# A hybrid decoder layer: the x1 transposes in the out projection and the first half of the MoBA keys' transposes move to other places

## The chip, the cores and the metric

The kernel runs on one NeuronCore of one Trainium2 chip. The metric is the device time of one execution in microseconds (us), the median of the runs. Lower is better.

## The reference

One decoder layer on a 256 x 1024 input. The projection `h @ w_in` gives queries, keys and values for two attention mixers (NSA with its compressed, selected and window branches, and MoBA), and gates; what the two mixers give is merged by gates and `w_out`, and a feed-forward part follows. The parts that the change touches:

```python
qkv = qkv_m.reshape(b, seq, 3, MOBA_HEADS, d)
qm = partial_rope(qkv[:, :, 0], cos, sin)
km = partial_rope(qkv[:, :, 1], cos, sin)
vm = qkv[:, :, 2]
y_moba = moba_attention(to_kv(qm), to_kv(km), to_kv(vm))
...
mixed = g_nsa * (y_nsa @ w_up_nsa[layer]) + g_moba * (y_moba @ w_up_moba[layer])
x = x + mixed @ w_out[layer]
h2 = rmsnorm(x, norm2_g[layer])
u = jax.nn.relu(h2 @ w_ff1[layer])
x = x + (u * u) @ w_ff2[layer]
```

With 256 tokens a MoBA block is the whole sequence, so MoBA is causal attention over 8 heads of 64.

## The kernel before

**Weights in 60 chunks.** All weights pass through in chunks of about 1 MB. Chunk c has a slot, slot c, in which TensorE (PE) multiplies with it. Each weight is split into two fp32r parts: ACT writes `whi`, a rounded copy (line 100), and DVE writes `wlo`, the rest (line 102). In slot c the split of chunk c+2 runs, in two halves (`split`), and SP's queue loads chunk c+5 (`load`). There are three buffers each of `raw`, `whi` and `wlo`.

**Triples of passes.** `mm3` makes three matmuls for each product: high by high, high by low, low by high; the first two have the same operand as weights. Here each of the three is called a pass. In slots 0 to 11 (`xstat`) the activations `hTh` and `hTl` are the weights and 512 columns of a chunk stream by: 24 passes a slot, numbered from 0, in triples (hTh, whi), (hTh, wlo), (hTl, whi). In the slots behind (`wstat`) the chunk's columns are the weights: (whi, high), (whi, low), (wlo, high), 48 passes of 256 columns a slot.

**Order by hand.** The program is written out in the order in which it is to run on each engine. `at(pos, f, ...)` puts a piece of other work at a share of a slot; `run_slot` sorts the pieces by share and issues each before the first pass i with pos <= i/n, where n is the number of passes. So pos 0.25 of 24 is ahead of pass 6, pos 0.48 ahead of pass 12. Every engine works off its own queue in that order; where one engine needs what another makes, it waits at the head of its queue.

**Slots 8 to 12, around the keys.** Slots 8 and 9 make the MoBA keys `km` (in the buffers `qtm`), slots 10 and 11 the values `vm`. The keys are rotated by DVE (`rope`, lines 276 to 279) in the middle of slot 10. In slot 11 `transp_heads` (lines 281 to 296) transposes them in two halves: four PE transposes (line 286) into one PSUM bank, then `split_evac`: ACT copies the bank to `kmh` (line 303) and `km` (line 304), and DVE subtracts to `kml` (line 305). From slot 11 on only the bank `tp` is left for this (`turn["tp"]`), so the two halves share it. The results are first read in slot 17. Also in slot 11, by share of the slot: the halves of the split's `whi` at 0.0 and 0.06 and of `wlo` at 0.09 and 0.46; at 0.1 the scores of attention unit 1 and the products of unit 0 on PE; at 0.11 unit 1's maxima on DVE (`d_max`, lines 440 to 446, first `Sa`, then `Sb`); at 0.12 unit 0's result (`d_yevac`, lines 506 and 507); at 0.5 the exponentials over `Sa` on ACT (`d_exp`, line 453) and the evacuation of the first `vm` bank (line 266); at 0.52 the exponentials over `Sb`. The norm of unit 1 (`d_norm`, line 458) follows in slot 12. Slot 12 begins the merge gates and writes the bank that the first `vm` evacuation frees.

**Slots 24 to 27, the out projection.** Slot 24+i makes two blocks of `mixed @ w_out`; its evacuation (`wout_evac`, lines 702 to 710) stands at the beginning of the next slot: DVE adds the blocks to x in `x1T`. In slot 25 `x1_rows` transposes the first two blocks of `x1T` into the bank `yb` (line 722), and ACT copies them out (line 724).

Of the kernel before, what the change touches and what calls it, by code (L numbers as in the profile page):

```python
# [40 lines left out]
def hybrid_layer(ctx: ExitStack, tc: tile.TileContext, gxd, w, w1c, small, const, gf, out):  # L41
# [14 lines left out]
    def bank(tag, name):  # L56
        return ps.tile([128, 512], F32, name=name, tag=tag)
# [8 lines left out]
    def acc_tile():  # L66
        return next_bank("acc")
# [4 lines left out]
    def s_tile(x):  # L72
        return ps_s.tile([128, 2, 512], F32, name="S" + "ab"[x])
# [113 lines left out]
    def at(pos, f, *a):  # L187
        ev.append((pos, f, a))

    def run_slot(mms):  # L190
        n = len(mms)
        es = sorted(ev, key=lambda e: e[0])
        ev.clear()
        j = 0
        for i, m in enumerate(mms):
            while j < len(es) and es[j][0] <= i / n:
                es[j][1](*es[j][2])
                j += 1
            m()
        while j < len(es):  # L200
            es[j][1](*es[j][2])
            j += 1
# [9 lines left out]
    def xstat(c, n, accs, kts):  # L212

        r = []
        h, l = hi[c], lo[c]
        order = [(t, k) for t in range(2) for k in range(4)]
        if c == 0:
            order.sort(key=lambda e: e[1])
        for t, k in order:
            kt = kts[k]  # L220
            if True:
                lh, ll = (a[:, kt, t * 128:(t + 1) * 128] for a in (hTh, hTl))
                r += mm3(accs[t][:, :n], lh, ll, h[:, k * n:(k + 1) * n],
                         l[:, k * n:(k + 1) * n], kt == 0, kt == 7)
        return r

    def wstat(o, c, off, nk, ncol, ah, al, ks=None, first=0, last=None):

        r = []
        last = nk - 1 if last is None else last  # L230
        for k in (range(nk) if ks is None else ks):
            a = k * ncol + off
            r += mm3(o, hi[c][:, a:a + 128], lo[c][:, a:a + 128], ah[:, k, :], al[:, k, :],
                     k == first, k == last)
        return r

    def split_events(c, hs, ls):
        for i in range(2):
            at(hs[i], split, c + 2, i, 2, "h")
        for i in range(2):  # L240
            if ls[i] <= 1:
                at(ls[i], split, c + 2, i, 2, "l")
        if ls[1] <= 1:
            at(max(ls) + 0.05, load, c + 5)

    def std_events(c):
        if 9 <= c < 20 and c % 2:
            split_events(c, (0.0, 0.06), (0.09, 0.46))
        elif 9 <= c < 20:
            split_events(c, (0.0, 0.45), (0.3, 0.8))  # L250
        else:
            split_events(c, (0.0, 0.45), (0.3, 0.46))
# [6 lines left out]
    tm = {"kva": kva, "kvb": kvb, "vm": vm}  # L259
# [47 lines left out]
    def qk_tiles(name, n, q):  # L307
        m = 128 if q else 256
        return (ap_.tile([128, n, 128], F32, name=name + "0"),
                ap_.tile([128, n, m], F32R, name=name + "h"),  # L310
                ap_.tile([128, n, m], F32R, name=name + "l"))
# [61 lines left out]
    qrT, qmT, kmT = (qk_tiles(n, 4, n != "km") for n in ("qr", "qm", "km"))  # L373
# [135 lines left out]
    def unit_events(s):  # L509
        d = (s - 9) // 2  # L510
        if not 9 <= s <= 21:
            return
        if s % 2 == 0:
            at(0.1, d_norm, d)
            at(0.78, d_trans, d)
            return
        if d < 6:
            at(0.1, d_scores, d)
        if d > 0:
            at(0.1, d_pv, d - 1)  # L520
        if d < 6:
            at(0.11, d_max, d)
            at(0.2 if s > 12 else 0.5, d_exp, d, 0)
            at(0.22 if s > 12 else 0.52, d_exp, d, 1)
        if d > 0:
            at(0.12, d_yevac, d - 1)
# [4 lines left out]
    for sec, c0, n in groups:  # L531
        if sec in ("q", "qm", "km"):
            tm[sec] = ap_.tile([128, 2, 512], F32, name="qtm", bufs=2)
        if sec == "kvb":
            accs = [s_tile(t)[:, 0] for t in range(2)]
        else:
            accs = [acc_tile(), acc_tile()]
        for i in range(2):
            c = c0 + i
            if c == 0:  # L540
                at(0.6, load, 5)
            elif c == 1:
                at(0.87, row_norm)
                for k in range(4):
                    at(0.88, split, 2, k, 4)
                for k in range(4):
                    at(1.1, split, 3, k, 4)
                at(1.2, load, 6)
            elif c == 2:
                split_events(c, (0.0, 0.3), (0.5, 0.8))  # L550
                at(0.3, cmp_gather, 0)
                at(0.55, cmp_gather, 1)
                at(0.7, rope, kva, 2)
            else:
                std_events(c)
            unit_events(c)
            if c == 3:
                at(0.65, cmp_mlp1)
                at(0.85, transp_k, kva, ksT)
            if c == 4:  # L560
                at(0.2, gate_evac)
                at(0.3, rope, kvb[:, :, 0:128], 2)
                at(0.4, cmp_mlp2)
            if c == 5:
                at(0.3, transp_k, kvb[:, :, 0:128], kwT)
            if c == 6:
                at(0.4, transp_heads, tm["q"], qT, 0)
                at(0.5, transp_heads, tm["q"], qT, 1)
                at(0.6, rope, tm["q"], 8)
            if c == 7:  # L570
                at(0.1, cmp_scores)
                at(0.4, transp_heads, tm["q"], qrT, 0)
                at(0.55, transp_heads, tm["q"], qrT, 1)
            if c == 8:
                at(0.35, cmp_probs_t)
                at(0.3, rope, tm["qm"], 8)
            if c == 9:
                at(0.3, transp_heads, tm["qm"], qmT, 0)
                at(0.45, transp_heads, tm["qm"], qmT, 1)
            if c == 10:  # L580
                at(0.5, rope, tm["km"], 8)
            if c == 11:
                turn["tp"] = ["tp"]
                at(0.25, transp_heads, tm["km"], kmT, 0, False)
                at(0.48, transp_heads, tm["km"], kmT, 1, False)
            if i == 1:
                at(1.0 if c == 1 else 0.5, evac_tm, sec, 0, accs[0], n)
                at(1.0, evac_tm, sec, 1, accs[1], n)
            run_slot(xstat(c, n, accs, range(4 * i, 4 * i + 4)))
# [122 lines left out]
    def lo_late(pos, c):  # L712
        for k in range(2):
            at(pos, split, c + 2, k, 2, "l")
        at(pos + 0.01, load, c + 5)

    def x1_rows(k2s, tiles):
        for k2, tp in zip(k2s, tiles):
            v = tp.rearrange("p (t d) -> p t d", t=2)
            for t in range(2):  # L720
                for m in range(2):
                    pe.transpose(v[:, t, m * 128:(m + 1) * 128],  # L722
                                 x1T[:, 2 * k2 + m, t * 128:(t + 1) * 128], ident)
            act.activation(FB["x1"][:, :, k2 * 256:(k2 + 1) * 256], v, AF.Copy)

    for i in range(4):
        c = C_WOUT + i
        if i == 0:
            lo_late(0.03, c - 1)
        split_events(c, (0.0, 0.1), ((0.5, 0.5), (0.3, 0.3), (0.3, 0.3), (9, 9))[i])  # L730
        for f, a in prev:
            at(0.02, f, *a)
        if i == 1:
            at(0.01, open_ff)
            at(0.5, lambda: x1_rows([0], [bank("yb", "yb")]))
            at(0.9, lambda: act.dma_start(FB["gfb"], gf[None, :].to_broadcast([128, 1024])))
        if i == 3:
            outs = [acc_tile()[:, 0:256] for _ in range(2)]
            at(0.52, wout_evac, i, outs, (0,))
            run_slot([m for j in range(2)  # L740
                      for m in wstat(outs[j], c, j * 128, 8, 256, mxh, mxl)])
            prev = [(wout_evac, (i, outs, (1,)))]
        else:
            mms, outs, _ = two_blocks(c, mxh, mxl, 6 if i == 0 else 8)
            run_slot(mms)
            prev = [(wout_evac, (i, outs))]
# [198 lines left out]
```

## Time and profile before

| | us |
|---|---|
| median of 3 runs | 392.18 |
| lowest and highest | 391.62, 392.22 |
| the profiled execution | 392.12 |
| its span, first to last instruction | 390.3 |
| PE busy in it | 377.5 (97%) |

Engines: PE is TensorE's matmul, PEld its weight load, DVE VectorE, ACT ScalarE, SP the queue of the loads. L286 is line 286 of the kernel. A matmul's row is longer than its step, since matmuls overlap: the distance from start to start is what it costs. In the PE rows the operands are named by the program's tiles, `acc<-whi,hTh`; which of them are the weights depends on the slot, as told above. Idle time that a row gives in brackets is that of its engine just before it, with the instruction that ended it.

### The profile page before, as it was taken

What the parts mean: (1) busy time and instruction counts of PE and PEld (TensorE: products, weight loads), DVE (VectorE), ACT (ScalarE), POOL (GpSimd) and SP (SyncE); (2) the same over time, 40 slices, a digit from 0 to 9 for tenths busy, and PEclk for the clock granted to TensorE, in tenths of its full rate; (3) what the DMA queues carried; (4) which work ended last, traced back from release to release, by engine and by line L of the source; (5) the groups of instructions that cost most, each with busy time, mean ns of one, the idle gap of its engine ahead of it and who ended that gap; (6) DMA issues with size and microseconds to landing.
All of it is one profiled execution on the core that took longest, in us unless ns stands there. A gap on an engine that the chain in (4) does not pass through costs nothing.

```text
span 390.3 us, 6512 instructions
## 1 busy us (share of the span) xinstructions
PE 377.5 (97%) x2687; PEld 343.7 (88%) x2687; DVE 261.1 (67%) x400; ACT 204.6 (52%) x358; POOL 10.0 (3%) x18
## 2 busy tenths in 40 slices
PE   6899999989999999999999999999999999999993
PEld 5688888868999999999999999999998888888883
DVE  5987487895978879867957666667567443344444
ACT  5565645747747467526445455555655464334412
POOL 5300000000000000000000000000000000000001
PEclk9999999999999999999999999999999999999998
DMA  7885625333335333632674546445645547455003
GB/s 237 316 346 219 216 107 192 132 107 111 109 109 191 128 115 107 217 118 99 233 252 160 188 196 216 174 158 209 213 145 183 214 154 275 165 177 200 0 2 107
DMA packets 11693, 66.33 MB, mean 170 GB/s; under 512 B 1296, under 2 KB 3600, under 8 KB 4368
## 3 DMA queue, kind: packets, MB, share of 16 engines
q1 hardware_dynamic: 11232, 65.14, 46.5%
q10 hardware_dynamic: 432, 0.79, 0.7%
q8 instruction: 21, 0.34, 0.3%
q14 instruction: 8, 0.07, 0.1%
HBM read 64.87 MB, written 1.05 MB: 169 GB/s over the span
## 4 chain that ended last, share of the span: by engine, by line
PE 87%; DVE 5%; issue 3%; ACT 2%; DMA 1%; SPq 0%; POOL 0%; POOLq 0%; DVEq 0%
PE acc L205 55%; PE o L205 21%; PE yb L205 2%; PE Sb L205 2%; PE Sa L205 2%; DVE wlo L102 1%; ACT P L453 1%; PE tp L205 1%; DMA gx<-in_gx_dram 1%; PE tp L286 1%; PE Sb L479 1%; PE Sa L479 1%; DVE hTl L162 1%; PE acc L722 0%; DVE P L467 0%
## 5 line engine op out<-in xcount | busy, mean ns | idle before, releaser
L100 ACT ACTIVATE whi<-raw 128x1024 fp32r<-128x1024 f32 (+2 forms) x128 | 123.8, 990 | 102.7 <-PE o L205 35.4
L102 DVE TENSOR_TENSOR wlo<-raw,whi 128x1024 fp32r<-128x1024 f32 (+2 forms) x128 | 145.1, 1165 | 43.7 <-ACT whi L100 43.6
L205 PE MATMUL acc<-h2h,whi 128*128 128x256 f32 x256 | 71.9, 281 | 0.0
L205 PE MATMUL acc<-h2l,whi 128*128 128x256 f32 x256 | 71.9, 281 | 0.0
L205 PE MATMUL acc<-h2h,wlo 128*128 128x256 f32 x256 | 71.9, 281 | 0.0
L205 PE MATMUL o<-whi,sqh 128*128 128x512 f32 (+1 forms) x128 | 49.5, 387 | 0.0
L205 PE MATMUL o<-whi,sql 128*128 128x512 f32 (+1 forms) x128 | 49.4, 386 | 0.0
L205 PE MATMUL o<-wlo,sqh 128*128 128x512 f32 (+1 forms) x128 | 49.4, 386 | 0.0
L205 PEld LDWEIGHTS acc<-h2h,whi 128*128 128x128 f32 x256 | 49.2, 192 | 0.0
L205 PEld LDWEIGHTS acc<-h2l,whi 128*128 128x128 f32 x256 | 48.1, 188 | 0.0
L205 PEld LDWEIGHTS acc<-h2h,wlo 128*128 128x128 f32 x256 | 48.0, 188 | 0.0
L205 PE MATMUL acc<-hTh,wlo 128*128 128x256 f32 x128 | 37.3, 291 | 0.0
L205 PE MATMUL acc<-hTh,whi 128*128 128x256 f32 x128 | 36.3, 283 | 0.4 <-ACT vm L266 0.4
L205 PE MATMUL acc<-hTl,whi 128*128 128x256 f32 x128 | 36.1, 282 | 0.0
L205 PE MATMUL acc<-wlo,hTh 128*128 128x512 f32 (+1 forms) x80 | 31.7, 397 | 3.4 <-DVE wlo L102 3.2
L205 PE MATMUL acc<-whi,hTh 128*128 128x512 f32 (+1 forms) x80 | 31.6, 395 | 0.0
L205 PE MATMUL acc<-whi,hTl 128*128 128x512 f32 (+1 forms) x80 | 30.7, 384 | 0.0
L205 PEld LDWEIGHTS o<-whi,sql 128*128 128x128 f32 x128 | 24.0, 188 | 4.9
L205 PEld LDWEIGHTS o<-whi,sqh 128*128 128x128 f32 x128 | 24.0, 188 | 4.9
L205 PEld LDWEIGHTS o<-wlo,sqh 128*128 128x128 f32 x128 | 24.0, 188 | 4.8
L205 PEld LDWEIGHTS acc<-hTh,whi 128*128 128x128 f32 x128 | 24.5, 191 | 0.9 <-ACT vm L266 0.8
L205 PEld LDWEIGHTS acc<-hTh,wlo 128*128 128x128 f32 x128 | 24.4, 191 | 0.8 <-issue 0.7
(243 smaller groups left out, 619.3 us busy)
## 6 DMA issues: line engine op xcount, KB each, us to landing
raw<-in_ff_dram SPq DMA_DIRECT2D x32, 1024.0 KB, 4.8
raw<-in_gm_dram SPq DMA_DIRECT2D x8, 1024.0 KB, 4.8
raw<-in_wout_dram SPq DMA_DIRECT2D x4, 1024.0 KB, 4.8
raw<-in_q_dram SPq DMA_DIRECT2D x2, 1024.0 KB, 6.2
raw<-in_qm_dram SPq DMA_DIRECT2D x2, 1024.0 KB, 5.8
raw<-in_km_dram SPq DMA_DIRECT2D x2, 1024.0 KB, 5.6
raw<-in_vm_dram SPq DMA_DIRECT2D x2, 1024.0 KB, 4.8
raw<-in_upn_dram SPq DMA_DIRECT2D x2, 1024.0 KB, 4.7
```

The lines of the kernel that those rows point to most:

```text
L100: act.activation(hi[c][:, a:b], raw[c][:, a:b], AF.Copy)
L102: dve.tensor_tensor(lo[c][:, a:b], raw[c][:, a:b], hi[c][:, a:b].bitcast(F32), op=ALU.subtract)
L162: dve.scalar_tensor_tensor(hTl[:, kt, :], xT[:, kt, :], g1[:, kt:kt + 1], hTh[:, kt, :].bitcast(F32), op0=ALU.mult, op1=ALU.subtract)
L205: pe.matmul(o, l, r, start=start, stop=stop, skip_group_check=True)
L286: pe.transpose(tp[:, j * 256 + t * 128:j * 256 + t * 128 + 128], src[:, t, (2 * i + j) * 128:(2 * i + j + 1) * 128], ident)
L453: act.activation(P[:, 2 * x + j, a:b], S[x][:, j, a:b], AF.Exp, scale=0.125, bias=st[:, 1, i:i + 1], accum_out=st[:, 2, i:i + 1])
L479: pe.transpose(S[x][:, j, c:c + 128], P[:, 2 * x + j, c:c + 128], ident)
```

## The change

The four x1 transposes of slot 25 move from 0.5 of the slot, ahead of pass 24 (the first of a triple), to 26/48 - 0.001, ahead of pass 26 (behind the second of a triple). The first half of the keys' transposes in slot 11 moves from 0.25, ahead of pass 6, to 0.02, ahead of pass 1: behind the first pass of the slot, behind the first half of the split's `whi`, and now ahead of the second half of `whi`, of both halves of `wlo`, of unit 1's scores and maxima and of unit 0's products and result. With the transposes move their ACT copies and their DVE subtraction. The second half stays at 0.48.

```diff
             if c == 11:
                 turn["tp"] = ["tp"]
-                at(0.25, transp_heads, tm["km"], kmT, 0, False)
+                at(0.02, transp_heads, tm["km"], kmT, 0, False)
                 at(0.48, transp_heads, tm["km"], kmT, 1, False)
...
         if i == 1:
             at(0.01, open_ff)
-            at(0.5, lambda: x1_rows([0], [bank("yb", "yb")]))
+
+            at(26 / 48 - 0.001, lambda: x1_rows([0], [bank("yb", "yb")]))
             at(0.9, lambda: act.dma_start(FB["gfb"], gf[None, :].to_broadcast([128, 1024])))
```

## Rows read from the trace of the kernel before

**Rows 1.** The page: busy us, share and instructions; then its chain by engine

```profile
PE 377.5 (97%) x2687; PEld 343.7 (88%) x2687; DVE 261.1 (67%) x400; ACT 204.6 (52%) x358; POOL 10.0 (3%) x18
...
PE 87%; DVE 5%; issue 3%; ACT 2%; DMA 1%; SPq 0%; POOL 0%; POOLq 0%; DVEq 0%
```

**Rows 2.** Stretches: length, busy us of PE, PEld, DVE, ACT, POOL, clock, DMA

```profile
60.00:92.00 32.00, 30.46 (x188) 24.02 (x187) 25.28 (x52) 19.57 (x50) 0.00 (x0) 1.00 0.44 148
92.00:184.00 92.00, 92.00 (x822) 88.39 (x822) 72.86 (x113) 54.11 (x120) 0.00 (x0) 1.00 0.37 132
184.00:206.00 22.00, 22.00 (x189) 22.00 (x189) 15.93 (x24) 11.21 (x17) 0.00 (x0) 1.00 0.63 216
```

**Rows 3.** Waits: engine, line, releaser: total us, times, longest

```profile
PEld tp L286 <- DVE kml L305: 1.6, 1, 1.6
```

**Rows 4.** Timeline, PE, slot 11: start, us, instruction, out<-in [idle before <-releaser]

```profile
80.47 0.40 PE L205 MATMUL acc<-whi,hTh 128*128 128x512 f32 x1
...
86.44 0.40 PE L205 MATMUL acc<-whi,hTl 128*128 128x512 f32 x1
...
87.96 0.66 PE L286 MATMUL tp<-ident,qtm 128*128 128x128 f32 x4 [1.12 <-DVE kml L305]
...
88.92 0.39 PE L205 MATMUL acc<-whi,hTl 128*128 128x512 f32 x1
...
90.96 0.39 PE L205 MATMUL acc<-whi,hTl 128*128 128x512 f32 x1
...
91.77 0.39 PE L205 MATMUL acc<-hTh,whi 128*128 128x256 f32 x1 [0.41 <-ACT vm L266]
```

**Rows 5.** Timeline, PE, slot 9, around a transposition behind a second pass

```profile
68.22 0.40 PE L205 MATMUL acc<-wlo,hTh 128*128 128x512 f32 x1
...
69.36 0.40 PE L205 MATMUL acc<-wlo,hTh 128*128 128x512 f32 x1
```

**Rows 6.** Timeline, DVE, slots 10 to 12

```profile
79.82 0.29 DVE L279 TENSOR_TENSOR qtm<-ropa,ropb 128x128 f32<-128x128 f32 x1
...
80.90 2.35 DVE L102 TENSOR_TENSOR wlo<-raw,whi 128x1024 fp32r<-128x1024 f32 x2
...
83.17 0.69 DVE L440 TENSOR_TENSOR Sa<-Sa,kc 128x512 f32<-128x512 f32 x1
...
84.95 0.17 DVE L446 TENSOR_SCALAR ust<-ust 128x4 f32<-128x4 f32 x1
...
87.22 0.68 DVE L305 TENSOR_TENSOR kml<-tp,kmh 128x512 fp32r<-128x512 f32 x1
...
89.56 0.69 DVE L305 TENSOR_TENSOR kml<-tp,kmh 128x512 fp32r<-128x512 f32 x1 [0.52 <-ACT km L304]
...
93.35 0.17 DVE L458 TENSOR_SCALAR ust<-ust 128x8 f32<-128x8 f32 x1 [3.10 <-ACT P L453]
```

**Rows 7.** Timeline, ACT, slot 11

```profile
80.71 2.01 ACT L100 ACTIVATE whi<-raw 128x1024 fp32r<-128x1024 f32 x2 [1.47 <-PE acc L205]
...
85.48 0.60 ACT L303 ACTIVATE kmh<-tp 128x512 fp32r<-128x512 f32 x1 [0.94 <-PE tp L286]
...
85.97 0.38 ACT L304 ACTIVATE km<-tp 128x256 f32<-128x256 f32 x1
...
89.41 0.37 ACT L453 ACTIVATE P<-Sa,ust 128x128 f32<-128x128 f32 x1
```

**Rows 8.** Timeline, PE, PEld and DVE, out projection, slot 25

```profile
187.95 0.28 PE L205 MATMUL acc<-mxh,whi 128*128 128x256 f32 x1
...
190.31 0.28 PE L205 MATMUL acc<-mxh,wlo 128*128 128x256 f32 x1
...
191.10 0.28 PE L205 MATMUL acc<-mxh,wlo 128*128 128x256 f32 x1
...
190.33 0.46 PEld L722 LDWEIGHTS yb<-ident,gx 128*128 128x128 f32 x4
...
189.57 0.75 DVE L702 TENSOR_TENSOR gx<-gx,acc 128x256 f32<-128x256 f32 x2
```

## The prediction

> **What bounds the kernel now.** I read the page's busy times and chain first: TensorE is busy for 97% of the span and carries 87% of the chain [rows 1]. So only time in which PE itself stands still, or extra work on PE, can move the end. The stretches then say where it stands still: from 92 to 206 us PE is busy without a gap, from 60 to 92 us it lacks 1.5 us, all at the full granted clock, 1.00 [rows 2]. The waits name the larger gap: the weight loads of the MoBA keys' transposes (line 286) waited once for DVE's `kml` (line 305), 1.6 us [rows 3]. The PE timeline of slot 11 shows it: pass 11 starts at 86.44, then nothing until 87.96, then four transposes; a smaller gap stands at the start of slot 12, at 91.77, behind ACT's evacuation of `vm` [rows 4].
>
> Why PE stood there follows from the two engines that empty the bank. In slot 11 both halves of the keys go through the one bank `tp`. The first half is read out by ACT (`kmh` at 85.48, `km` at 85.97) [rows 7] and by DVE (`kml`), and DVE has `kml` queued behind the whole maximum of the next attention unit, which holds it from 83.17 to 87.22 [rows 6]. The second half's transposes can only start when `kml` is over, at 87.90. They are also at the head of PE's queue, so passes 12 to 23, which need nothing from that bank, wait with them.
>
> **Part 1, the keys' first half, from pass 6 to pass 1 of slot 11.** No instruction is added; four transposes, two ACT copies and one DVE subtraction move forward on their queues, and no DMA is issued by them.
>
> The stall's size: from pass 11 to pass 14 it takes 88.92 - 86.44 = 2.48 us [rows 4]. The same pattern without a wait (three steps and four transposes) is in slot 9: 69.36 - 68.22 = 1.14 [rows 5]. The stall is 1.34 us. One step of a 512-column pass is (90.96 - 88.92)/9 = 0.227 [rows 4], so four transposes cost 1.14 - 3 x 0.227 = 0.46, paid in the old place and in the new one; with the move pass 11 still starts at 86.44.
>
> On PE in the new place: the transposes follow pass 0, at 80.47 + 0.23 = 80.70 [rows 4], their weights a step earlier, at 80.47. They read the rotated keys, whose last DVE instruction ends at 79.82 + 0.29 = 80.11 [rows 6]: 0.36 us to spare. The bank was last used two slots before.
>
> On ACT: the first half of the weights' split stands ahead, from 80.71, 1.0 us a half [rows 7]. Then `kmh` starts at 81.71, `km` at 82.20 and ends at 82.58. The second half of that split goes back by about 0.9 us; it is needed two slots later.
>
> On DVE: `kml` waits for `km` too, as its second instance does (0.52 us for ACT's `km`) [rows 6]. So it runs from 82.61 to 83.29. In the queue it now stands between the two subtractions that begin at 80.90, 2.27 us for both up to 83.17, 1.13 each [rows 6]. The second of them, and the maximum behind it, begin at 83.29 + 1.13 = 84.42 instead of 83.17: 1.25 us later. That is the cost of the move, and it has cover. The first exponentials, which need the maximum of `Sa`, ran at 89.41 [rows 7] because ACT had the second half's copies ahead of them; that maximum's last instruction ends at 84.95 + 0.17 = 85.12 [rows 6], then at 86.37.
>
> What the bank is worth: free at 83.29, it is wanted at 86.44. So the second half's transposes start a step after pass 11, at 86.67, and pass 14 at 88.92 - 1.34 = 87.58. What is late next is the same evacuation of `vm`: behind it are copies and exponentials that all hang on the second half's transposes, and these come earlier by the same amount, so slot 12 begins at 91.77 - 1.34 = 90.43, with its gap as before. The exponentials begin at 89.41 - 1.34 = 88.07, 1.70 us after the delayed maximum. DVE's next work, the norm at 93.35, had waited 3.10 us for ACT [rows 6], so 1.25 us of delay are gone before it. From there on PE has no gap to lose the gain in [rows 2], and DVE and ACT follow PE. SP's load of a later chunk, released by DVE's second subtraction of the slot, may go out about half a microsecond later; its chunk is split three slots on.
>
> Two bounds. The new place lies between a first and a second pass, the row lies behind a second pass; I take equal cost, zero, and at most one step, +0.23. And the gap at slot 12, 91.77 - 90.96 - 0.23 = 0.58 us, could go as well if ACT gets ahead: -0.58. I take zero, since nothing ahead of that evacuation on ACT becomes shorter.
>
> Every matmul has a weight load of its own here, 2687 of each [rows 1], so transposes between two passes with the same weights add no load. The Trainium skill (TensorE: Matmul & The Clock Gate, Part 2, Step-by-step: what each phase is for) says that weights typically stay put across many matmuls and are loaded once; by that rule passes 0 and 1, which share `hTh`, would be parted and one load more be paid, at most a step, and the time would be 391.07 us. The trace speaks against it.
>
> **Part 2, the four x1 transposes, from pass 24 to pass 26 of slot 25.** Nothing else lies between the two places. Their price in the old place: 191.10 - 190.31 = 0.79 us for three steps and four transposes; a step is (190.31 - 187.95)/20 = 0.118, so 0.79 - 0.35 = 0.44 [rows 8]. Behind a second pass it was 0.46 [rows 5]. So the place is worth nothing, within 0.02 either way. Their input comes from two DVE additions that end at 189.57 + 0.75 = 190.32; the first weight load of the four came at 190.33 [rows 8]. The second of the four is the first to need the second addition, at 190.33 + 0.46/4 = 190.44, so in this execution nothing waited, with about a tenth to spare; two passes later it has 0.24 more. I take 0.00, as bounds -0.05 and +0.02.
>
> **Sum.** -1.34 + 0.00 = -1.34 us. The profiled execution took 392.12 us for a span of 390.3; it becomes 390.78. The median of the runs shown, 392.18, is 0.06 above it: 390.84, which I give as 390.8.
>
> **The rivals.**
> Rival A, the keys come late: if the rotation ends after 80.47, PE stands at pass 1 with all of slot 11 behind it, one for one. For: only 0.36 us of margin, behind a busy DVE. Against: DVE and PE have both been led by ACT since slot 10, and the margin is one of the trace. With the rotation 0.9 us later it gives 390.84 + 0.54 = 391.4; all gain is gone at 1.7.
> Rival B, slower than before: the maximum on DVE. `kml` now holds it up, and `kml` hangs on ACT. If `kml` began more than 1.70 us after 82.61, the exponentials, the evacuation of `vm` and slot 12 would come late one for one; from 1.70 + 1.34 = 3.04 us on the kernel is slower. With `kml` at 86.65 (4.04 later): 392.18 + 1.00 = 393.2. Against: ACT has only the split ahead of `kmh`; even with both halves ahead, `kmh` starts at 82.72, 1.0 us later, still hidden.
> Rival C, the gain is given back downstream: some DVE or ACT step that does not follow PE becomes late. Against: no gap of PE after 92 us [rows 2]; for: x1 had a tenth to spare. Half given back is 391.5.
> Rival D, the change does not do what it says: the second half waited not for the bank but for something else on DVE, and the stall stays: 392.2. For: DVE's next instruction starts at the same moment; against: the rotation was over 7 us before, so the bank is the only thing left that `kml` holds.
>
> **How the numbers follow.** Forecast 0.80 (390.8, own range 390.2 to 391.1), A 0.06, B 0.03, C 0.06, D 0.05. The range starts at 390.84 - 0.58 - 0.05 = 390.2 and goes up to 391.6, which takes in the extra step, the middle of A and half of C. About 0.2% (0.78 us, above 391.4 for the end of faster) is what a measurement can tell from no change. Faster: the forecast and a part of A and C, 0.85; same: the rest of A and C, and D, 0.12; slower: B, 0.03.
>
> **What would show it.** Right: no wait of line 286 on `kml`; the second half's transposes at about 86.7; `kml` first at about 82.6 and the maximum on `Sa` at about 84.4; slot 12 from about 90.4, still released by ACT's `vm`; the x1 transposes between a pass on `mxl` and one on `wlo`, near 189.3. Wrong: PE idle before the first transposes of slot 11 (A), a gap before slot 12 wider by what was saved (B), a new PE wait after 92 us (C), line 286 still idle at 86.7 (D).

## The result, and the profile after

The changed kernel takes 387.33 us, the median of four runs (386.57 to 387.94), against 392.2 before (391.62 to 393.21): the ratio is 0.9872 with the interval 0.9843 to 0.9901. Forecast were 390.8 us and a range of 390.2 to 391.6. The direction was right, and the time is 3.5 us below the forecast, outside the range. The profiled execution has a span of 384.8 us, 5.5 less than that of before.

The page's busy times and its chain by engine:

```profile
PE 374.4 (97%) x2687; PEld 341.7 (89%) x2687; DVE 260.9 (68%) x400; ACT 204.9 (53%) x358; POOL 9.8 (3%) x18
...
PE 91%; issue 3%; DVE 2%; ACT 1%; DMA 1%; SPq 0%; POOL 0%; POOLq 0%; DVEq 0%
```

PE is still busy for 97% of the span, now of a shorter one: 374.4 us in place of 377.5 [rows 1], with the same 2687 matmuls. So it isn't only idle time that went; the same matmuls take less time. The waits of PE (engine, line, releaser: total us, times, longest):

```profile
PE acc L205 <- DVE wlo L102: 1.9, 2, 1.2
PE yb L115 <- POOL ones L111: 1.4, 1, 1.4
PE tp L331 <- ACT kcd L263: 0.4, 1, 0.4
PE acc L205 <- ACT vm L266: 0.4, 1, 0.4
```

Line 286 no longer waits for `kml`, neither here nor among the waits of the weight loads, where [rows 3] had it; the wait on `vm` at slot 12 is there as before.

**Slot 11 went as worked out.** This execution reaches slot 11 0.29 us earlier than the one of before (80.18 in place of 80.47). It is 0.30 us ahead at the chain's first passes already (15.70 in place of 16.00), so 0.29 is no work of the change and is to be taken off each forecast moment. The PE timeline:

```profile
80.18 0.40 PE L205 MATMUL acc<-whi,hTh 128*128 128x512 f32 x1
...
80.42 0.60 PE L286 MATMUL tp<-ident,qtm 128*128 128x128 f32 x4
...
81.09 0.40 PE L205 MATMUL acc<-whi,hTl 128*128 128x512 f32 x1
...
86.18 0.40 PE L205 MATMUL acc<-whi,hTl 128*128 128x512 f32 x1
...
86.42 0.60 PE L286 MATMUL tp<-ident,qtm 128*128 128x128 f32 x4
...
89.38 0.39 PE L205 MATMUL acc<-whi,hTl 128*128 128x512 f32 x1
...
90.16 0.39 PE L205 MATMUL acc<-hTh,whi 128*128 128x256 f32 x1 [0.39 <-ACT vm L266]
```

The first transposes follow pass 0. Pass 11 starts at 86.18, the second transposes at 86.42 without idle time (forecast 86.67 - 0.29 = 86.38), and slot 12 at 90.16 (forecast 90.43 - 0.29 = 90.14), with 0.39 us behind ACT's `vm` as before [rows 4]. DVE and ACT in the same stretch:

```profile
82.28 0.69 DVE L305 TENSOR_TENSOR kml<-tp,kmh 128x512 fp32r<-128x512 f32 x1 [0.46 <-ACT km L304]
...
84.02 0.69 DVE L440 TENSOR_TENSOR Sa<-Sa,kc 128x512 f32<-128x512 f32 x1
...
85.80 0.17 DVE L446 TENSOR_SCALAR ust<-ust 128x4 f32<-128x4 f32 x1
...
91.76 0.17 DVE L458 TENSOR_SCALAR ust<-ust 128x8 f32<-128x8 f32 x1 [1.86 <-ACT P L453]
```

```profile
81.39 0.58 ACT L303 ACTIVATE kmh<-tp 128x512 fp32r<-128x512 f32 x1
...
87.81 0.37 ACT L453 ACTIVATE P<-Sa,ust 128x128 f32<-128x128 f32 x1
```

`kml` waits for `km` and runs at 82.28 (forecast 82.32), the maximum on `Sa` begins at 84.02 (84.13), and its last instruction at 85.80 ends 1.84 us ahead of the exponentials at 87.81. DVE's norm still waits 1.86 us for ACT at 91.76, where it had waited 3.10 [rows 6]. The delay of the maximum is covered. From 91.77 to 90.16, less 0.29 of the earlier start, is 1.32 us of gain: the forecast's 1.34.

**The rest lies behind the x1 transposes.** The chain in order of time (start, us, what, count of instructions), of the kernel before and then of the changed one, from slot 21 to the first block of ff2:

```profile
165.54 25.05 PE acc L205 x211
...
190.59 0.44 PE yb L722 x4
...
191.03 104.59 PE acc L205 x888
...
295.62 8.21 PE o L205 x36
```

```profile
163.94 25.29 PE acc L205 x213
...
189.23 0.44 PE yb L722 x4
...
189.66 100.43 PE acc L205 x886
...
290.10 8.18 PE o L205 x36
```

The first row of each is the stream of passes ahead of the x1 transposes: 211 passes in 25.05 us, 213 in 25.29, the same 0.1187 us a pass (its beginning included). The third is the stream from behind them to the end of ff1: 888 passes in 104.59 us, 117.8 ns each, become 886 in 100.43, 113.3 ns each. That is 4.4 ns less for every pass, 3.9 us in all, with the same shapes and operands. It lasts for 100 us, over the rest of slot 25, two more slots of the out projection and sixteen of ff1. The granted clock was the same. Stretches, as in [rows 2], before and after (the share behind the clock is DMA's):

```profile
206.00:290.00 84.00, 84.00 (x715) 84.00 (x715) 55.99 (x61) 45.97 (x61) 0.00 (x0) 1.00 0.52 188
```

```profile
190.00:290.00 100.00, 100.00 (x885) 100.00 (x884) 68.36 (x80) 56.45 (x75) 0.00 (x0) 1.00 0.58 205
```

PE is busy for the whole of both, at the clock 1.00. The weight loads of ff1 show the two steps (count, then shortest/median/longest in ns), before and after:

```profile
L205 PEld LDWEIGHTS acc<-h2h,whi x227: 192/192/192, 204.9 to 284.7; 128*128 128x128 f32 x114
L205 PEld LDWEIGHTS acc<-h2l,whi x227: 187/188/188, 205.0 to 284.9; 128*128 128x128 f32 x114
L205 PEld LDWEIGHTS acc<-h2h,wlo x227: 187/188/188, 205.1 to 285.0; 128*128 128x128 f32 x114
```

```profile
L205 PEld LDWEIGHTS acc<-h2h,whi x242: 187/188/188, 202.8 to 284.7; 128*128 128x128 f32 x121
L205 PEld LDWEIGHTS acc<-h2l,whi x242: 187/188/188, 202.9 to 284.8; 128*128 128x128 f32 x121
L205 PEld LDWEIGHTS acc<-h2h,wlo x242: 187/188/188, 203.0 to 284.9; 128*128 128x128 f32 x121
```

Before, one weight load of every triple takes 192 ns, always that of the first pass; the other two take 188. After, all take 188.

The sum of the spans: -0.29 at the start, -1.32 in slot 11, +0.24 for the two passes that now lie ahead of the x1 transposes, and -4.15 from 104.59 to 100.44 (start to start of ff2), of which 0.24 is those two passes again: -5.5 us. Medians of runs give 4.9. The start's 0.3 belongs to the execution (another one of the same kernel, the last experiment, ends slot 21's products at 164.19 in place of 163.94); the rest lies within the spread of the executions.

### The profile page after: what moved, and what is told of

It reads as the page before. It is cut to its first block, busy times and chain, and to the rows that moved or that the text cites. A ratio compares the mean times of both kernels' runs of the same rounds, so it can differ in the third digit from the quotient of the medians.

```text
span 384.8 us, 6512 instructions
## 1 busy us (share of the span) xinstructions
PE 374.4 (97%) x2687; PEld 341.7 (89%) x2687; DVE 260.9 (68%) x400; ACT 204.9 (53%) x358; POOL 9.8 (3%) x18
## 4 chain that ended last, share of the span: by engine, by line
PE 91%; issue 3%; DVE 2%; ACT 1%; DMA 1%; SPq 0%; POOL 0%; POOLq 0%; DVEq 0%
PE acc L205 58%; PE o L205 21%; PE yb L205 3%; PE Sb L205 2%; PE Sa L205 2%; PE tp L205 1%; DMA gx<-in_gx_dram 1%; PE Sa L479 1%; PE Sb L479 1%; PE tp L286 1%; DVE wlo L102 1%; DVE hTl L162 1%; ACT P L453 0%; PE acc L722 0%; POOL rstd L182 0%
## 5 line engine op out<-in xcount | busy, mean ns | idle before, releaser
L205 PE MATMUL acc<-h2h,whi 128*128 128x256 f32 x256 | 70.7, 276 | 0.0
L205 PE MATMUL acc<-h2l,whi 128*128 128x256 f32 x256 | 70.7, 276 | 0.0
L205 PE MATMUL acc<-h2h,wlo 128*128 128x256 f32 x256 | 70.7, 276 | 0.0
L205 PEld LDWEIGHTS acc<-h2h,whi 128*128 128x128 f32 x256 | 48.1, 188 | 0.0
L205 PE MATMUL acc<-whi,hTl 128*128 128x512 f32 (+1 forms) x80 | 31.5, 393 | 0.0
```

Of the source, the lines that this page charges most:

```text
L205: pe.matmul(o, l, r, start=start, stop=stop, skip_group_check=True)
```

## The experiments

Eighteen runs: the two parts alone, then kernels that move, split or leave out interruptions of the stream of passes, and the changed kernel once more. I call an interruption any other PE work between two passes; the short step is 113.3 ns, the long step 117.8 ns (the expectations call them fast and slow). Steps are read from the chain's rows, us by count, from behind the x1 transposes to the end of ff1. Where no ratio is given, the kernel was executed once, and the kernel before, executed beside it, took from 391.55 to 394.13 us; there the verdict rests on the step in the trace, and the time only has to agree with it.

**One part alone: x1.** Edit, on the kernel before:

```diff
-            at(0.5, lambda: x1_rows([0], [bank("yb", "yb")]))
+            at(26 / 48 - 0.001, lambda: x1_rows([0], [bank("yb", "yb")]))
```

> The kernel before with the x1 transposes alone moved, ahead of pass 26 of slot 25. Theory P (place): the stream of 256-column passes has two steady steps, 113.3 ns and 117.8 ns, and the place of the last interruption in the triple decides between them; some 888 passes from the x1 transposes to the end of ff1 take 4.5 ns less each, so 4.0 us less than before, 388.2 us, with PE's wait of line 286 on kml still there. Theory K (the keys' move shifts the later work against something and that makes the passes faster): no change, 392.2 us, step 117.8 ns. Theory T (the moment, not the place): as P.

388.38 us, ratio 0.9897 (0.9868 to 0.9926): 3.9 us less. The step is 113.3 ns (886 passes in 100.43 us), and PE's old wait is there:

```profile
PE tp L286 <- DVE kml L305: 1.1, 1, 1.1
```

The x1 move makes the larger part alone. Theory K falls.

**One part alone: the keys.** Edit, on the kernel before:

```diff
-                at(0.25, transp_heads, tm["km"], kmT, 0, False)
+                at(0.02, transp_heads, tm["km"], kmT, 0, False)
```

> The kernel before with the keys' first half alone moved. Theory P: only the stall on kml goes, -1.3 us, 390.9 us, the step stays 117.8 ns in the out projection and ff1. Theory K: all of the gain, 387.3 us, step 113.3 ns. Theory T: as P.

390.87 us, ratio 0.9962 (0.9943 to 0.998): 1.4 us less, and the step is 117.8 ns (888 passes in 104.59 us). This is what I had forecast for the whole change. The two parts add up, 3.9 + 1.4 = 5.3 us against 4.9 for both, within the intervals.

**One pass later.** Edits on the changed kernel from here on:

```diff
-            at(26 / 48 - 0.001, lambda: x1_rows([0], [bank("yb", "yb")]))
+            at(27 / 48 - 0.001, lambda: x1_rows([0], [bank("yb", "yb")]))
```

> The changed kernel with the x1 transposes one pass later, ahead of pass 27, between two triples again. Theory P: the slow step is back, 117.8 ns, about 391.0 us. Theory T (it is enough that they come later than before, clear of DVE's additions): step 113.3 ns, 387.3 us.

391.4 us, 117.8 ns (885 passes in 104.23 us). Coming later than DVE's additions isn't what helps; theory T falls.

**Three passes later**, 29 / 48 in place of 26 / 48.

> The changed kernel with the x1 transposes ahead of pass 29, behind the second pass of the next triple. Theory P: step 113.3 ns, 387.3 us. A theory by which only the very moment ahead of pass 26 is good: 117.8 ns, 391.0 us.

387.58 us, 113.3 ns (883 passes in 100.09 us): the next triple's same place gives the same.

**One pass earlier**, 25 / 48.

> The changed kernel with the x1 transposes ahead of pass 25, behind the first pass of a triple, so that the next weights are the same whi as those of the pass ahead. Theory P1 (any place inside a triple gives the fast step): 113.3 ns, 387.3 us. Theory P2 (only behind the second pass, where the next weights are wlo): 117.8 ns, 391.0 us.

386.48 us, 113.3 ns (887 passes in 100.54 us). P1 as far as this goes: of the three places only the one between two triples gives the long step.

**No interruption in slot 25.** Edit:

```diff
-            at(26 / 48 - 0.001, lambda: x1_rows([0], [bank("yb", "yb")]))
...
-            at(0.5, x1_rows, range(1, 4), [acc_tile() for _ in range(3)])
+            at(0.5, x1_rows, range(4), [bank("yb", "yb")] + [acc_tile() for _ in range(3)])
```

> The changed kernel without an interruption in slot 25: these four x1 transposes join the twelve others in slot 45. Theory P (an interruption sets the state and it holds until the next one): the slow step that the stream has since slot 21 holds to the end of ff1, 117.8 ns, about 391.0 us. Rival (the stream falls into the fast step by itself when operands change at a slot's beginning, and the old place of the transposes was what spoiled it): 113.3 ns from slot 28 at the latest, at most 387.7 us.

391.21 us. The chain has one unbroken row of passes from slot 21 to the end of ff1:

```profile
164.67 129.63 PE acc L205 x1099
```

118.0 ns each (beginning included), the long step throughout. So the stream has it ahead of slot 25 already and keeps it while the activations change three times, from `yThn` over `yThm` and `mxh` to `h2h`, up to the 512-column passes of ff2; in the changed kernel it is the interruption that ends it. The four transposes cost 0.44 us in either place; in the right one they save 3.9.

**Another interruption moved.** In the kernel before the step is short in slot 20 and long from slot 21 on: there the sixteen narrow matmuls of unit 5's products stand ahead of pass 5. Weight loads of the kernel before, in slot 20 and from slot 22 on:

```profile
L205 PEld LDWEIGHTS acc<-yTln,whi x9: 187/188/188, 158.0 to 160.7; 128*128 128x128 f32 x9
```

```profile
L205 PEld LDWEIGHTS acc<-yTlm,whi x32: 192/192/192, 170.6 to 181.6; 128*128 128x128 f32 x32
```

Edit, with 0.06 for pass 3 and then 0.08 for pass 4:

```diff
-            at(0.1, d_pv, d - 1)
+            at(0.1 if s < 21 else 0.06, d_pv, d - 1)
```

> The changed kernel with another interruption moved: the products of attention unit 5 in slot 21, behind whose second pass of a triple (pass 4) the step goes from 113.3 to 117.8 ns in both kernels, now stand behind a third pass (pass 2). If the place in the triple decides for this interruption too, the step may stay at 113.3 ns in slots 21 to 25, some 211 passes, -0.9 us: 386.4 us. If an interruption by these narrow matmuls always leads to the slow step: 387.3 us.

> As the run before, but behind a first pass (pass 3). Fast in slots 21 to 25: 386.4 us; slow: 387.3 us. From there the x1 transposes behind a second pass either keep a fast stream fast or, if they only toggle the state, make it slow: then 391.0 us or more.

Ahead of pass 3: 387.07 us, 113.3 ns behind x1. Ahead of pass 4: 390.88 us, 117.8 ns behind x1, although the x1 transposes stand where the changed kernel has them. In both the step in slots 21 to 25 is the long one, so the 0.9 us hoped for there didn't come, and the second run's 390.88 is not the 387.3 expected for that case. So the place in the triple alone doesn't decide: what the x1 transposes do depends on where the products stood. The loads show a phase: the 192 ns load in slots 22 to 25 is the second pass's with the products ahead of pass 5, the third's ahead of pass 3, the first's ahead of pass 4. Theory R was formed on this.

**Two kernels to tell R from P.** Edits: products ahead of pass 4 and x1 ahead of pass 27; products ahead of pass 3 and x1 ahead of pass 25.

> The changed kernel with unit 5's products behind a first pass (as two runs before, which makes the first pass of each triple the one with the long weight load in slots 21 to 25) and the x1 transposes ahead of pass 27, between two triples, the place that gave the slow step when the long load was the second pass's. Theory R (what decides is the place of the interruption counted from the pass with the long load: slow if the next pass is two behind it, fast if it is that pass or the one behind it): next pass is the first, the long load's own, so fast, 113.3 ns, 387.1 us. Theory P (the place in the triple alone): between triples is slow, 117.8 ns, 391.0 us.

> The changed kernel with unit 5's products behind a third pass (the long load is then the third pass's) and the x1 transposes ahead of pass 25, the place that was fast when the long load was the second pass's. Theory R: the next pass, the second, is two behind the third, so slow, 117.8 ns with the long load on the second pass, about 391.0 us. Theory P: fast, 387.0 us.

The first: 387.13 us, 113.3 ns. The second: 391.31 us, 117.8 ns; its long load, in the out projection ahead of x1 and then in ff1:

```profile
L205 PEld LDWEIGHTS acc<-mxh,wlo x17: 192/192/192, 181.3 to 186.9; 128*128 128x128 f32 x17
```

```profile
L205 PEld LDWEIGHTS acc<-h2l,whi x224: 192/192/192, 206.0 to 284.8; 128*128 128x128 f32 x112
```

Both as R has it, the new phase too, and against P: between two triples is now good, and the place that had been good is bad.

**The products in two interruptions.** Edit, with 8 and then with 7:

```diff
-            at(0.1, d_pv, d - 1)
+            at(0.1, d_pv, d - 1, (0, 1) if s < 21 else (0,))
+            if s == 21:
+                at(8 / 48 - 0.001, d_pv, d - 1, (1,))
```

(`d_pv` gets the list of the halves to do, and in slot 21 `d_yevac` moves from 0.12 to 0.18.)

> The changed kernel with unit 5's products in two interruptions of eight narrow matmuls, ahead of pass 5 and ahead of pass 8 of slot 21. Theory R, if it holds for narrow matmuls too: the first leaves the long load on the second pass, the second one's next pass is one behind it, so the step is 113.3 ns from slot 21 on, 0.9 us less than the changed kernel, 386.4 us. If these narrow matmuls lead to the slow step whatever the state ahead of them: 387.4 us.

> As the run before with the second interruption ahead of pass 7, whose next pass is the one with the long load itself. Theory R for narrow matmuls: fast from slot 21 on, 386.4 us; otherwise 387.4 us.

With 8: 386.33 us, the short step both ahead of and behind x1. With 7: 390.58 us. Its chain, ahead of x1 and behind it:

```profile
164.79 24.11 PE acc L205 x211
...
189.74 104.35 PE acc L205 x886
```

211 passes at 114.3 ns (their beginning included), then 886 at 117.8 ns: the second interruption brought the short step, and the x1 transposes ended it. I had not expected that; R, which needs a long load to count from, says nothing on a stream without one. What all kernels so far have in common is the number of passes between the last interruption and the x1 transposes, which the chain's rows count:

| kernel | passes since the last interruption | over a multiple of 3 | step behind x1, ns |
|---|---|---|---|
| before; keys alone | 211 | 1 | 117.8 |
| changed; x1 alone | 213 | 0 | 113.3 |
| x1 ahead of 25 | 212 | 2 | 113.3 |
| x1 ahead of 27 | 214 | 1 | 117.8 |
| x1 ahead of 29 | 216 | 0 | 113.3 |
| products ahead of 3 | 215 | 2 | 113.3 |
| products ahead of 4 | 214 | 1 | 117.8 |
| products 4, x1 27 | 215 | 2 | 113.3 |
| products 3, x1 25 | 214 | 1 | 117.8 |
| products split, 8 | 210 | 0 | 113.3 |
| products split, 7 | 211 | 1 | 117.8 |

One over a multiple of three: the long step; else the short one. That is theory D. It holds for the split products themselves (3 passes, then 2: short both times).

**Two kernels on D.** Edits: two of the four x1 transposes ahead of pass 26 and two ahead of pass 27; then five transposes ahead of pass 26, the first made twice.

> The changed kernel with the four x1 transposes in two interruptions, two ahead of pass 26 and two ahead of pass 27. Theory D (what decides is how many passes lie between one interruption and the next, counted modulo three: one over a multiple gives the slow step, none or two the fast one, also where the stream in between is fast): the second has one pass ahead of it since the first, so slow, 117.8 ns, 391.0 us. Theory R alone (slow only if a long load is there to be placed against, and a fast stream stays fast): 113.3 ns, 387.3 us.

> The changed kernel with five transposes ahead of pass 26 in place of four (one of them made twice, 0.1 us). Theory D counts passes of the stream only: fast, 113.3 ns, 387.4 us. Rival N (all matmuls count, the interruption's too, so that a fifth transposition shifts the phase by one): one over, slow, 117.8 ns, 391.1 us.

The first: 390.81 us, 117.8 ns, as D has it (one pass). But its long load is the second pass's, where every other interruption by x1 that led to the long step left it on the pass just behind itself:

```profile
L205 PEld LDWEIGHTS acc<-h2l,whi x224: 192/192/192, 205.9 to 284.7; 128*128 128x128 f32 x112
```

So D names the step here and not the phase; one pass may be too few for the stream to settle between the two, and this kernel alone doesn't carry the verdict on R. The run with 7 does. The second: 387.19 us, 113.3 ns. A fifth transposition changes nothing, so it isn't counted; N falls. R would have the same here, so this run doesn't part D from R.

**The gate slots.** In slots 12 to 19 of the kernel before, the first nine or so loads behind the products take 186 to 189 ns, and then, with no interruption between, all are long:

```profile
L205 PEld LDWEIGHTS acc<-hTh,whi x14: 192/192/192, 107.8 to 112.5; 128*128 128x128 f32 x14
```

The loads of the other two passes of the triple are the same.

Edit: scores and products of slots 13 to 19 at 0.08 (pass 4), then at 0.06 (pass 3), in place of 0.1.

> The changed kernel with the scores and products of the attention units in slots 13, 15, 17 and 19 ahead of pass 4 in place of pass 5. In these slots the step is 120 ns with a long load in every pass. If that is a third state that a place can leave too: 113.3 or 117.8 ns in up to 324 passes, -0.7 to -2.1 us, 385.2 to 386.6 us. If it belongs to the operands of this stage (hTh, hTl): 387.3 us.

> As the run before, ahead of pass 3. The same two outcomes: 385.2 to 386.6 us if a place can leave the 120 ns step, 387.3 us if it belongs to the operands of the stage.

386.52 and 386.77 us, beside the changed kernel's 386.57 to 387.94. By time alone this would not decide, since 386.52 also lies in the range of the first outcome; the trace does. A stretch between two interruptions, of the changed kernel and of the first of these:

```profile
101.51 9.90 PE acc L205 x81
```

```profile
101.34 10.02 PE acc L205 x82
```

122.2 ns a pass in both (beginning included). The place of these interruptions doesn't change the gate slots' step. It ends at slot 20, with the change of operands from `hTh` to `yThn` and without an interruption. That the operands cause it was not tried. The count of D doesn't run through these slots either: with 81, 82 and 83 passes from the products of slot 19 to the transposes of slot 20, the loads behind these settle at 187 to 188 ns each time, those of the short step, though 82 is one over a multiple.

**The split products, timed beside the changed kernel.**

> The kernel with unit 5's products in two interruptions (ahead of pass 5 and of pass 8 of slot 21), timed: 113.3 ns in slots 21 to 27 and ff1, 0.9 us less than the changed kernel for some 200 passes of 4.5 ns less, 386.4 us. By a theory that the split costs as much as it gives: as the changed kernel.

> The changed kernel itself, timed on the same chip as the run before: 387.3 us, the split version 0.9 us below it.

386.67 us, ratio 0.9864 (0.985 to 0.9878), beside 387.01, ratio 0.9881 (0.9861 to 0.9901): 0.3 us where 0.9 was expected, and the intervals overlap, so by time it is unclear. The traces tell where the rest is. The chains of the split version and of the changed kernel around slots 21 to 25:

```profile
164.91 24.02 PE acc L205 x210
...
188.93 0.29 PE yb L726
...
189.77 100.43 PE acc L205 x886
```

```profile
164.19 25.29 PE acc L205 x213
...
189.48 0.44 PE yb L722 x4
...
189.92 100.43 PE acc L205 x886
```

The 210 passes take 24.02 us; 213 at the changed kernel's 0.1187 took 25.29, so about 0.9 us are saved on equal counts. The x1 transposes then stand from 188.93 to 189.77, 0.84 us in place of 0.44. On PE and DVE:

```profile
188.89 0.88 PE L726 MATMUL yb<-ident,gx 128*128 128x128 f32 x4
```

```profile
188.42 0.75 DVE L706 TENSOR_TENSOR gx<-gx,acc 128x256 f32<-128x256 f32 x2
```

DVE's additions end at 188.42 + 0.75 = 189.17, and the transposes, which begin at 188.89, have to wait for the second one. PE had become faster than the DVE queue ahead of it, and 0.40 us of the gain are gone there. The products themselves, of the split version and then of the changed kernel:

```profile
162.76 0.80 PE yb L205 x8
163.56 0.55 PE acc L205 x3
164.11 0.80 PE yb L205 x8
```

```profile
162.75 1.45 PE yb L205 x16
```

The two halves and the three passes between take 2.15 us, where the whole and three passes at 0.1187 take 1.81: another 0.34. What is left is 0.91 - 0.40 - 0.34 = 0.17 us, and the two profiled executions, 386.67 and 386.85, differ by 0.18. Three passes later (which the count allows) the x1 transposes would be clear of this; that was not tried.

## Why the prediction was wrong

**Right: part 1.** Each step of it is in the trace of after, to about 0.1 us: stall, queue positions, cover, and the unchanged wait at slot 12. Alone it measured 1.4 us (390.87) where 1.34 was forecast. Equal cost for the transposes between a first and a second pass was right too: 80.18 to 81.09 is two steps and four transposes, 0.91, where 0.46 and two steps of 0.227 make 0.91. Neither bound was needed, and none of the rivals occurred: PE's waits after 92 us are those of before (C), and the other three would have shown in slots 11 and 12.

**Wrong: part 2, the sentence "So the place is worth nothing, within 0.02 either way."** What I priced was the four transposes, from the pass ahead of them to the third behind, and that price is indeed the same: 0.44 us in both kernels. What I did not price was the stream behind them. I took the step of a 256-column pass, 0.118, for a fixed property of the shape, and it isn't one: behind the interruption the same passes run at 113.3 or at 117.8 ns, and over 886 of them that is 3.9 us. The term that failed is "part 2 = 0.00"; it measured -3.9 us in the kernel with x1 alone.

**The rivals lacked it.** All four were about waits, and the premise ahead of them, "So only time in which PE itself stands still, or extra work on PE, can move the end", left nothing to gain where PE has no gap [rows 2]. A busy engine was taken for one at its limit. The trace of before held the sign against it: in slot 20 loads of 188 ns only, from slot 21 on one in three at 192, for the same shapes, with an interruption between. Two levels of the step within one kernel, divided by an interruption, are a rival for any change that moves an interruption: in that trace the passes start 113.3 ns apart late in slot 20 and 117.8 behind the x1 transposes, 4.4 ns before rounding, by 888 passes, 3.9 us, and downwards, since the stream behind the x1 transposes had the long loads already. With it the range would have gone down to about 386.9, 3.9 us below the forecast.

**What stays open.** What in the chip makes the stream remember a count of three is not shown. The triples themselves have a period of three in their operands, so whether it is three matmuls, or the three operands, was not parted. D holds for the x1 transposes in every kernel here, but it isn't a general rule: unit 5's undivided products, 13, 14 or 15 passes behind the transposes of slot 20, led to the long step in all three places, where D has the short one for 14 and 15, and it fails across the gate slots. D was found on the kernels of the table. Of the two tests behind it, five transposes speak against N but not for D over R, and the transposes ahead of 26 and 27 gave D's step but not the phase of the other kernels. So what is shown is that the place of the x1 transposes, counted from the interruption ahead of it, decides the 3.9 us in all these kernels; why it does is open.

## What to carry to other kernels

A stream of matmuls that shows no gap can still run at more than one steady step; compare the time per pass and the length of the weight loads between stretches of the same shape before taking PE's busy time for a floor. When a change moves other PE work into or within such a stream, price the stream behind it as well as the work itself, and look at places one and two passes away: they cost nothing to try. And a PE that becomes faster meets the next queue: a place that had a tenth of a microsecond to spare was late by 0.40 us as soon as the stream ahead of it sped up.

## What the runs showed of the hardware

A weight load of 128 x 128 in this stream takes 188 or 192 ns, and the step of the 256-column passes is 113.3 ns where all loads take 188 and 117.8 ns where one in three takes 192. In the gate slots, where all take 192 from about the tenth pass behind the products on, the passes are 122.2 ns apart on average, their slower beginning included. The long step held for 1099 passes (130 us) and three changes of the activations in the kernel without an interruption in slot 25; a stretch with interruptions took the short or the long step behind them, by their place. The step of the gate slots ended with a change of operands alone. Four transposes cost 0.44 us in the out projection wherever they had nothing to wait for and 0.46 in slot 11, and the granted clock was 1.00 in these stretches, before [rows 2] and after.
